# Two-layer hybrid decoder on one core: SwiGLU chunks in the order 2,4,4,4,4,4 instead of 4,4,4,4,4,2, with the gate tiles in a pool of their own

## The chip, the cores and the metric

The kernel runs on one core of one Trainium2 chip, as one program with one launch. The metric is device time in microseconds (us) from the start to the end of an execution; lower is better. The engines are named as in the profile: PE is the matmul engine (TensorE), PEld its weight loads, DVE is VectorE, ACT is ScalarE, POOL is GpSimd, and SP is SyncE, whose queue (SPq) issues nearly all DMA transfers here. psd, psy, wl, xL and the like are names of tiles in the program.

## The reference, cut to what matters

Two layers (DEPTH = 2) act on a prompt of 1024 tokens and on 8 sample tokens with the same weights. In each layer a projection of the normalised activations feeds differential attention and gated linear attention (GLA); both are run over the prompt, and for the 8 samples as a decode step over 64 pages of a key and value cache and a GLA state. Then follow the output projection and the part that the change is in:

```python
x = x + concat(attention, gla) @ w_out              # 1024 -> 1024
n = rmsnorm(x, norm2)
g, u = split(n @ w_gu)                              # 1024 -> 2 x 2816
x = x + (silu(g) * u) @ w_down                      # 2816 -> 1024
```

After the second layer x is written out as y_prompt and y_sample. Inputs, weights and outputs are float32. The kernel splits each float32 operand into a rounded high part and a remainder (wh and wl, hh and hl, xH and xL) and sums three matmuls, high by high, high by low and low by high.

## The kernel before

**Layout.** Activations lie features by tokens: x is 8 tiles (index j) of 128 features x 1032 tokens. The second part of a layer is done in two halves of the tokens: X = 0 has 512 prompt tokens, X = 1 the other 512 and the 8 sample tokens (520 columns, done as two matmuls of 260 columns). Each half runs `out_half` (output projection, residual, next x) and then `ffn_half`. While X = 0 runs, `decode` is interleaved with it: pages of the cache are loaded (`load_page`), multiplied on POOL (tile page) and summed on DVE (tile sall).

**The FFN.** The 2816 = 22 x 128 hidden rows are handled in chunks. `gates(c)` computes silu of the gate part into a tile sa, `ups(c)` multiplies the up part by it and leaves a pair of activation tiles hh and hl for each 128 rows, `down(c)` multiplies these by w_down and adds the result to acc. The chunks are pipelined: ups(c), gates(c+1), down(c); the last ups stands before the second-last down, so that the last two downs run back to back. PE sums into the pool psD of two buffers (psd); for X = 0 one buffer holds a pair of j, for X = 1 one j. One j of a down needs 3 matmuls of 512 columns for each 128 rows of the chunk (6 of 260 for X = 1), one cast of its weight block to wh on ACT and one subtraction to wl on DVE (`prep_tile`, three raw, three wh and two wl buffers), and, once per psd, the addition acc<-psd,acc on DVE.

**What stands at the end of a half.** In the last down of layer 0 each finished j goes to `new_x`: xH on ACT, xL on DVE, a square on ACT, and its addition to ssq on POOL. In the last down of layer 1 each finished j goes out instead: four transposes on PE (psy), a copy on ACT into yall, and a 256 KB store on SP (L1074). yall uses the place of sa, and ysall that of tb (same tags, one buffer each).

**The next half.** `out_half` for X = 1 loads two tiles oHa and oLa (1 MB each, SP, L967) and makes two more, oHb and oLb, from og on ACT and DVE. They are 128 x 2080 floats each, and the three matmuls of each of the eight k use b tiles first and a tiles second.

**What sets the order.** Calls carry a planned time (`dense`, `mix`), from which the build orders the instructions of each engine; an engine then runs its list in order, and each instruction waits for its inputs and for the place it writes to. A pool opened where a closed one lay takes over the same memory, and its tiles wait until the old tiles' last readers are done (reuse_waits); of a store the last reader is the transfer itself. The pool fp (sa, tb, hh, hl) stays open for X = 0 until out_half of X = 1 is done (`fctx`), while acc and the decode's tiles are closed right after X = 0 (`actx`).

Of the kernel before, what the change touches and what calls it, by code (L numbers as in the profile page):

```python
# [10 lines left out]
F32 = mybir.dt.float32  # L11
F32R = mybir.dt.float32r
# [50 lines left out]
def hybrid_kernel(  # L63
# [201 lines left out]
    def layer(l):  # L265
        sn = smp.tile([NB, 2 * H], F32, name="sn", tag="sn")
        osf = smp.tile([P, 2 * H, NB], F32, name="osf", tag="osf")
        smc = smp.tile([P, 2, 3, NB], F32, name="smc", tag="smc")
        gsm = smp.tile([P, H, NB], F32, name="gsm", tag="gsm")
        if l:  # L270
            sample_cols()

        with ExitStack() as octx:
            with ExitStack() as mix_:
                pgp = mix_.enter_context(tc.tile_pool(name="pgp", bufs=1, reuse_waits="tile", side="right"))
                with ExitStack() as dctx:
                    wa2 = phase_d(l, dctx, sn, pgp)
                ogb = octx.enter_context(tc.tile_pool(name="ogb", bufs=1, reuse_waits="tile"))
                og1 = ogb.tile([P, H, WM], F32, name="og1", tag="og1")
                oga = octx.enter_context(ExitStack())  # L280
                ogp = oga.enter_context(tc.tile_pool(name="oga", bufs=1, reuse_waits="tile"))
                og0 = ogp.tile([P, H, HALF], F32, name="og0", tag="og0")
                ogs = (og0, og1)
                with ExitStack() as gctx:
                    phase_g(l, gctx, ogs, smc, gsm, wa2)
            with ExitStack() as pctx:
                psD = pctx.enter_context(tc.tile_pool(name="psD", bufs=2, space=PSUM, reuse_waits="tile"))
                psn = pctx.enter_context(tc.tile_pool(name="psn", bufs=2, space=PSUM, reuse_waits="tile"))
                psX = pctx.enter_context(tc.tile_pool(name="psX", bufs=2, space=PSUM, reuse_waits="tile"))
                wps = [pctx.enter_context(tc.tile_pool(name=n, bufs=1, reuse_waits="tile", side="right")) for n in ("wFr", "wFh", "wFl")]  # L290
                span_start()
                with ExitStack() as fctx:
                    with ExitStack() as actx:
                        ac = new_acc(actx)
                        cp = actx.enter_context(tc.tile_pool(name="dec", bufs=1, reuse_waits="tile", side="right"))
                        acc = out_half(l, 0, og0, osf, ac, wps, psD)
                        oga.close()
                        ffn_half(l, 0, acc, ac, wps, psD, psn, fctx)
                        clock["mix"] = MIX_START
                        decode(l, cp, osf, smc, gsm, psX)  # L300
                    actx = pctx.enter_context(ExitStack())
                    ac = new_acc(actx)
                    acc = out_half(l, 1, og1, osf, ac, wps, psD)
                ffn_half(l, 1, acc, ac, wps, psD, psn, actx)
                span_end()

    def load_page(dst, src, idx):
# [685 lines left out]
                    new_x(acc, ac, X, j, g2c[:, l, j:j + 1])  # L993
        return acc

    def ffn_half(l, X, acc, ac, wps, psD, psn, st):
        W = COLS[X]
        t0 = X * HALF
        last = l == DEPTH - 1
        fp = st.enter_context(tc.tile_pool(name="fp", bufs=1, reuse_waits="tile"))  # L1000
        xh = lambda k: xH[:, k, t0:t0 + W]
        xl = lambda k: xL[:, k, t0:t0 + W]
        chunks = [list(range(c, min(c + 4, NF))) for c in range(0, NF, 4)]
        r = rstd[:, t0:t0 + W].unsqueeze(1)

        def gates(c):
            sa = fp.tile([P, 4, WM], F32, name="sa", tag="sa", bufs=1)
            for fs in groups(X, chunks[c]):
                ps = psD.tile([P, 2, 512], F32, name="psd", tag="d")
                for u, ff in enumerate(fs):  # L1010
                    dense(5.6)
                    ws = prep_tile(wps, w_gu[l, :, ff * P:(ff + 1) * P], KD)
                    gemm3(unit_outs(ps, X, u), *ws, xh, xl, range(KD))
                if fs[0] == 0:
                    rms_half(X, psn)
                n = len(fs)
                i0 = fs[0] - chunks[c][0]
                tt(unit_view(sa[:, i0:i0 + n, :W], X, n), unit_ps(ps, X, n),
                   unit_view(bc(r, [P, n, W]), X, n), ALU.mult)
            n = len(chunks[c])  # L1020
            last_silu.append(act(sa[:, :n, :W], sa[:, :n, :W], AF.Silu))
            if X == 0 or c == len(chunks) - 1:
                load_ln_exp()
            return sa

        def ups(c, sa):
            hs = []
            for fs in groups(X, chunks[c]):
                ps = psD.tile([P, 2, 512], F32, name="psd", tag="d")
                for u, ff in enumerate(fs):  # L1030
                    dense(5.6)
                    ws = prep_tile(wps, w_gu[l, :, DFF + ff * P:DFF + (ff + 1) * P], KD)
                    gemm3(unit_outs(ps, X, u), *ws, xh, xl, range(KD))
                n = len(fs)
                i0 = fs[0] - chunks[c][0]
                g = 2 if X == 0 else 1
                tb = fp.tile([P, g, W], F32, name="tb", tag="tb", bufs=1)[:, :n, :]
                tt(unit_view(tb, X, n), unit_ps(ps, X, n), unit_view(bc(r, [P, n, W]), X, n), ALU.mult)
                tt(tb, tb, sa[:, i0:i0 + n, :W], ALU.mult)
                hh = fp.tile([P, g, W], F32R, name="hh", tag="hh", bufs=6 // g)[:, :n, :]  # L1040
                hl = fp.tile([P, g, W], F32R, name="hl", tag="hl", bufs=6 // g)[:, :n, :]
                act(hh, tb, AF.Copy)
                tt(hl, tb, f(hh), ALU.subtract)
                for u in range(n):
                    hs.append((hh[:, u, :], hl[:, u, :]))
            return hs

        def down(c, hs):
            fs = chunks[c]
            end = c == len(chunks) - 1  # L1050
            if end and last:
                yall = fp.tile([P, 4, WM], F32, name="yall", tag="sa", bufs=1)
                ysall = fp.tile([P, 2 if X == 0 else 1, W], F32, name="ysall", tag="tb", bufs=1)
            for js in groups(X, list(range(KD))):
                ps = psD.tile([P, 2, 512], F32, name="psd", tag="d")
                for u, j in enumerate(js):
# [37 lines left out]
    def decode(l, cp, osf, smc, gsm, psX):  # L1094
# [25 lines left out]
        def sample_gla(p):  # L1120
            q, k, eg = (smc[:, p, a, :] for a in range(3))
            sh = [P, 4, DV]
            vbs = []
            for b0 in (0, 4):
                bs = slice(b0, b0 + 4)
                S0 = cp.tile(sh, F32, name="S0", tag="S0", bufs=1)
                vb = cp.tile(sh, F32, name="vb", tag="vb", bufs=2)
                mix(5)
                with behind(1):
                    for e in range(2):  # L1130
                        h = 2 * p + e
                        SP.dma_start(S0[64 * e:64 * e + 64], state_gla[l, bs, h].rearrange("b d v -> d b v"))
                        SP.dma_start(vb[64 * e:64 * e + 64],
                                     scr_gv[l][bs, h * DV:(h + 1) * DV].unsqueeze(0).to_broadcast([64, 4, DV]))
                tt(S0, S0, bc(eg[:, bs].unsqueeze(2), sh), ALU.mult, POOL)
                tt(vb, vb, bc(k[:, bs].unsqueeze(2), sh), ALU.mult, POOL)
                tt(S0, S0, vb, ALU.add, POOL)
                with tc.issue_after(mark_at(clock["mix"] + 10)[1].ins):
                    for e in range(2):
                        SP.dma_start(gla_sample[l, bs, 2 * p + e].rearrange("b d v -> d b v"), S0[64 * e:64 * e + 64])  # L1140
                tt(vb, S0, bc(q[:, bs].unsqueeze(2), sh), ALU.mult, POOL)
                vbs.append(vb)

            def out():
                ps = psx("pss")
                pv = ps[:, 0:16].rearrange("p (b e) -> p b e", e=2)
                for b in range(NB):
                    mm(pv[:, b, :], vbs[b // 4][:, b % 4, :], hsel, True, True)
                DVE.tensor_copy(osf[:, H + 2 * p:H + 2 * p + 2, :], pv.rearrange("p b e -> p e b"))

            return out

        def decode_softmax():
# [27 lines left out]
            for j in range(NPG):  # L1181
                mm(pw[:, j * 32:(j + 1) * 32], pe_[j // 4][:, (j % 4) * P:(j % 4 + 1) * P], sel, True, True)
            act(wall, pw[:, 0:256].rearrange("p (j c) -> p j c", c=32), AF.Copy)
            wn = cp.tile([64, P], F32, name="dwn", tag="wn")
            DVE.tensor_copy(wn, bc(sm[:, 2:3], [64, P]))
            pn = psx("psn2")
            mm(pn[:, 0:32], wn, sel, True, True)
# [145 lines left out]
```

## Time and profile before

| | us |
|---|---|
| device time, median of 3 runs | 2788.39 (2784.14 to 2790.25) |
| device time of the profiled execution | 2795.14 |
| its span, first to last instruction | 2793.3 |
| PE busy | 2709.5 (97%) |
| DVE busy | 1824.9 (65%) |
| ACT busy | 1358.8 (49%) |
| POOL busy | 403.0 (14%) |
| mean granted TensorE clock | 0.989 |

The span starts with the first instruction, and all stamps below count from there; 1.8 us of the profiled execution lie around it. In it the last down of X = 0 ends near 974 us in layer 0 and near 2355 us in layer 1; those of X = 1 end near 1415 us and at the end of the span. A row of windows gives the stretch, its length, the busy time (and count) of PE, PEld, DVE, ACT and POOL, the granted TensorE clock (1.00 is 2.4 GHz, 0.50 is 1.2 GHz), the DMA engines' busy share and GB/s.

### The profile page before, as it was taken

How to read it: one execution, taken by the hardware profiler on the slowest of the kernel's cores; microseconds unless marked ns; L12 is line 12 of the kernel's file. 1: busy time of each engine (PE TensorE's matmuls, PEld its weight loads, DVE VectorE, ACT ScalarE, POOL GpSimd, SP SyncE). 2: the span in 40 equal slices, each digit the busy share in tenths (PEclk: the TensorE clock that was granted, in tenths of full speed). 3: DMA queues.
4: the chain of work that ended last, by engine and by line, in shares of the span. 5: the costliest groups of instructions: out<-in, count | busy, mean ns of one | idle time of the engine just before them, and what ended most of it. 6: DMA issues, size and time to landing. Idle time of an engine off the chain costs nothing.

```text
span 2793.3 us, 46822 instructions
## 1 busy us (share of the span) xinstructions
PE 2709.5 (97%) x16906; PEld 2403.9 (86%) x16906; DVE 1824.9 (65%) x3549; ACT 1358.8 (49%) x3343; POOL 403.0 (14%) x333
## 2 busy tenths in 40 slices
PE   8999999999999999999999999999999999999999
PEld 6888788777888799999988878877788888999999
DVE  6777676788777664444477775777777775544444
ACT  7888545533454442222278884455324454322222
POOL 1000100145343100000020001002453430000000
PEclk9999999999999999999999999999999999999999
DMA  5111111356666342333212111124566665333332
GB/s 133 56 56 41 57 32 54 109 176 201 185 200 195 104 128 84 93 94 94 75 42 70 47 38 49 32 59 137 174 202 177 191 192 151 91 92 91 91 91 84
DMA packets 461322, 298.13 MB, mean 107 GB/s; under 512 B 34698, under 2 KB 416906, under 8 KB 461090
## 3 DMA queue, kind: packets, MB, share of 16 engines
q1 hardware_dynamic: 452322, 290.90, 35.4%
q10 hardware_dynamic: 8704, 4.20, 0.6%
q8 instruction: 134, 2.20, 0.3%
q14 instruction: 98, 0.80, 0.1%
q0 software_dynamic: 64, 0.03, 0.0%
HBM read 271.53 MB, written 23.53 MB: 106 GB/s over the span
## 4 chain that ended last, share of the span: by engine, by line
PE 78%; DVE 10%; ACT 8%; issue 2%; DMA 2%; SPq 0%; POOL 0%; ACTq 0%; DVEq 0%; POOLq 0%
PE psd L82 56%; PE psq L82 4%; PE psqk L82 3%; PE psv L82 3%; PE psgg L82 2%; PE po L82 2%; ACT sc L88 2%; PE psA L82 1%; DVE wl L135 1%; PE psS L82 1%; ACT qn L88 1%; PE poG L82 1%; ACT qhh L88 1%; PE tpw L85 1%; DVE acc L135 1%
## 5 line engine op out<-in xcount | busy, mean ns | idle before, releaser
L88 ACT ACTIVATE wh<-raw 128x512 fp32r<-128x512 f32 (+1 forms) x608 | 353.6, 615 | 909.3 <-PE psd L82 737.3
L82 PE MATMUL psd<-xH,wh 128*128 128x260 f32 (+1 forms) x2112 | 681.9, 323 | 3.6 <-ACT xH L88 3.5
L82 PE MATMUL psd<-xL,wh 128*128 128x260 f32 (+1 forms) x2112 | 679.9, 322 | 4.2 <-DVE xL L138 4.2
L82 PE MATMUL psd<-xH,wl 128*128 128x260 f32 (+1 forms) x2112 | 682.2, 323 | 0.9 <-DVE wl L135 0.9
L135 DVE TENSOR_TENSOR wl<-raw,wh 128x512 fp32r<-128x512 f32 (+1 forms) x608 | 443.9, 746 | 72.8 <-issue 41.3
L82 PEld LDWEIGHTS psd<-xL,wh 128*128 128x128 f32 x2112 | 400.2, 189 | 38.4 <-DVE xL L138 6.5
L82 PEld LDWEIGHTS psd<-xH,wh 128*128 128x128 f32 x2112 | 399.8, 189 | 36.3 <-ACT xH L88 4.4
L82 PEld LDWEIGHTS psd<-xH,wl 128*128 128x128 f32 x2112 | 400.3, 190 | 34.2 <-DVE wl L135 1.8
L82 PE MATMUL psd<-hh,wl 128*128 128x260 f32 (+1 forms) x1056 | 340.6, 323 | 6.1 <-DVE wl L135 6.0
L82 PE MATMUL psd<-hh,wh 128*128 128x260 f32 (+1 forms) x1056 | 338.8, 321 | 0.9 <-DVE acc L135 0.9
L82 PE MATMUL psd<-hl,wh 128*128 128x260 f32 (+1 forms) x1056 | 338.3, 320 | 0.0
L135 POOL TENSOR_TENSOR page<-page,qbd 128x512 f32<-128x512 f32 x128 | 190.5, 1504 | 307.9 <-DMA page<-in_cache_k 162.7
L135 DVE TENSOR_TENSOR acc<-psd,acc 128x520 f32<-128x520 f32 (+1 forms) x144 | 125.6, 872 | 150.7 <-PE psd L82 150.7
L82 PEld LDWEIGHTS psd<-hh,wl 128*128 128x128 f32 x1056 | 199.1, 189 | 25.8 <-DVE wl L135 12.0
L82 PEld LDWEIGHTS psd<-hh,wh 128*128 128x128 f32 x1056 | 199.2, 189 | 14.6 <-issue 1.3
L82 PEld LDWEIGHTS psd<-hl,wh 128*128 128x128 f32 x1056 | 198.8, 188 | 13.6
L82 PE MATMUL psq<-wh,xH 128*128 128x384 f32 (+1 forms) x512 | 180.0, 352 | 7.3 <-DVE zs L135 4.3
L135 DVE TENSOR_TENSOR sa<-psd,rstd 128x520 f32<-128x520 f32 (+1 forms) x66 | 57.7, 874 | 197.0 <-PE psd L82 194.7
L82 PE MATMUL psq<-wh,xL 128*128 128x384 f32 (+1 forms) x512 | 179.4, 351 | 0.0
L82 PE MATMUL psq<-wl,xH 128*128 128x384 f32 (+1 forms) x512 | 178.6, 349 | 0.0
L135 DVE TENSOR_TENSOR tb<-psd,rstd 128x520 f32<-128x520 f32 (+1 forms) x66 | 57.7, 874 | 165.9 <-PE psd L82 165.9
L138 DVE SCALAR_TENSOR_TENSOR wl<-raw,g1c,wh 128x256 fp32r<-128x256 f32 (+2 forms) x160 | 80.9, 536 | 73.5 <-ACT wh L88 72.8
(330 smaller groups left out, 5421.2 us busy)
## 6 DMA issues: line engine op xcount, KB each, us to landing
raw<-in_w_gu SPq DMA_DIRECT2D x176, 512.0 KB
raw<-in_w_down SPq DMA_DIRECT2D x160, 256.0 KB
page<-in_cache_k SPq DMA_DIRECT2D x128, 256.0 KB
page<-in_cache_v SPq DMA_DIRECT2D x128, 256.0 KB
raw<-in_w_out SPq DMA_DIRECT2D x32, 512.0 KB
raw<-in_w_in SPq DMA_DIRECT2D x64, 192.0 KB
raw<-in_w_in SPq DMA_DIRECT2D x64, 128.0 KB
xt<-in_x_prompt SPq DMA_DIRECT2D x8, 512.0 KB
```

Of the source, the lines that this page charges most:

```text
L82: PE.matmul(out, lhsT=lhsT, rhs=rhs, start=start, stop=stop, skip_group_check=True)
L85: PE.matmul(out, lhsT=in_, rhs=ident[:n, :n], is_transpose=True)
L88: return ACT.activation(out, in_, func, **kw)
L135: return (eng or DVE).tensor_tensor(out, a, b, op=op)
L138: (eng or DVE).scalar_tensor_tensor(out=out, in0=in0, scalar=scalar, in1=in1, op0=op0, op1=op1)
```

## The change

The chunk of 2 x 128 rows, which was the last, becomes the first; the last two downs are both 4 x 128 rows deep. As the last two chunks of activations are held together, hh and hl have room for eight 128-row tiles instead of six. sa and tb (and with them yall and ysall) move from fp to a new pool fs, which for X = 0 is closed with actx, so before out_half of X = 1, and lies above fp. In decode the state S0 and the small tile dwn take slots of the tag page (five buffers) instead of places of their own. The matmuls, the weights loaded, and the other transfers are the same in number and size, except that the 128 x 256 weight blocks come first.

```diff
-                        ffn_half(l, 0, acc, ac, wps, psD, psn, fctx)
+                        ffn_half(l, 0, acc, ac, wps, psD, psn, fctx, actx)
...
-                ffn_half(l, 1, acc, ac, wps, psD, psn, actx)
+                ffn_half(l, 1, acc, ac, wps, psD, psn, actx, actx)
...
+        fs_ = st2.enter_context(tc.tile_pool(name="fs", bufs=1, reuse_waits="tile"))
...
-        chunks = [list(range(c, min(c + 4, NF))) for c in range(0, NF, 4)]
+        chunks = [list(range(max(0, c), c + 4)) for c in range(NF % 4 - 4, NF, 4)]
...
-            sa = fp.tile([P, 4, WM], F32, name="sa", tag="sa", bufs=1)
+            sa = fs_.tile([P, 4, WM], F32, name="sa", tag="sa", bufs=1)
...
-                hh = fp.tile([P, g, W], F32R, name="hh", tag="hh", bufs=6 // g)[:, :n, :]
+                hh = fp.tile([P, g, W], F32R, name="hh", tag="hh", bufs=8 // g)[:, :n, :]
...
-                yall = fp.tile([P, 4, WM], F32, name="yall", tag="sa", bufs=1)
+                yall = fs_.tile([P, 4, WM], F32, name="yall", tag="sa", bufs=1)
...
-                S0 = cp.tile(sh, F32, name="S0", tag="S0", bufs=1)
+                S0 = cp.tile([P, 512], F32, name="S0", tag="page", bufs=NPB).rearrange("p (b d) -> p b d", b=4)
```

**DVE, layer 0, the last down of X = 0.** Before, from the third addition to acc to the first two subtractions of the next output projection (wl<-raw,wh 128x512):

```order
L135 TENSOR_TENSOR acc<-psd,acc 128x2x512
L135 TENSOR_TENSOR xL<-acc,xH 128x512
L135 TENSOR_TENSOR wl<-raw,wh 128x256
L135 TENSOR_TENSOR xL<-acc,xH 128x512
L135 TENSOR_TENSOR wl<-raw,wh 128x256
L135 TENSOR_TENSOR xL<-acc,xH 128x512
L135 TENSOR_TENSOR acc<-psd,acc 128x2x512
L135 TENSOR_TENSOR wl<-raw,wh 128x256
L135 TENSOR_TENSOR xL<-acc,xH 128x512
```

The same stretch now, up to the last addition to acc:

```order
L135 TENSOR_TENSOR acc<-psd,acc 128x2x512
L135 TENSOR_TENSOR wl<-raw,wh 128x512
L135 TENSOR_TENSOR xL<-acc,xH 128x512
L135 TENSOR_TENSOR wl<-raw,wh 128x512
L135 TENSOR_TENSOR xL<-acc,xH 128x512
L135 TENSOR_TENSOR wl<-raw,wh 128x512
L135 TENSOR_TENSOR acc<-psd,acc 128x2x512
L135 TENSOR_TENSOR wl<-raw,wh 128x512 x2
L135 TENSOR_TENSOR xL<-acc,xH 128x512 x2
```

The same kinds of instruction alternate, but the weight blocks are twice as wide and one subtraction for the output projection has moved ahead of the last addition to acc.

**SP, layer 1, the end of X = 0.** Names in brackets are what the instruction waits for: DMAHW with a number is the landing of an earlier transfer, the others are engines. Before, the loads of oHa and oLa stand among the loads for the last down, and the stores of y (out<-yall) come behind them:

```order
L900 DMA raw<-in_w_down 128x2x128 [waits DMAHW6_49,DVE_49,Activation_49]
L967 DMA oHa<-scr_oh_110 128x4x512 [waits PE_49,Pool_49]
L900 DMA raw<-in_w_down 128x2x128 [waits DMAHW7_49,DVE_49,Activation_49]
L967 DMA oLa<-scr_ol_114 128x4x512
L900 DMA raw<-in_w_down 128x2x128 [waits DMAHW0_49,DVE_49,Activation_49]
```

Now the last two stores and what follows them:

```order
L1075 DMA out<-yall 128x4x128 [waits Activation_49]
L1075 DMA out<-yall 128x4x128 [waits DMAHW4_49,Activation_49]
L900 DMA raw<-in_w_out 128x8x128 [waits DMAHW6_49,DMAHW5_49,DVE_49]
L967 DMA oHa<-scr_oh_110 128x4x512 [waits DMAHW3_49,DMAHW4_49,DMAHW1_49,DMAHW0_49]
L967 DMA oLa<-scr_ol_114 128x4x512 [waits DMAHW7_49,PE_49,Pool_49]
L900 DMA raw<-in_w_out 128x8x128 [waits DVE_49]
```

oHa and oLa have moved behind all eight stores of y, and oHa waits for the landing of the last four. In layer 0 (no stores there) the two loads keep their place among the loads for the last down, and oHa waits for nothing.

**PE, the same place.** Now, from the last matmul of the last down over the last transposes to the first matmul that reads oHa (20 more rows of oHb and oLb lie between the two pieces):

```order
L82 MATMUL psd<-hl,wh 128x512
L82 MATMUL psd<-hh,wl 128x512
L85 MATMUL psy<-ident,acc 128x128 x8
L82 MATMUL psd<-oHb,wh 128x260 x2
L82 MATMUL psd<-oLb,wh 128x260
```

```order
L82 MATMUL psd<-oHb,wl 128x260
L82 MATMUL psd<-oHa,wh 128x260
L82 MATMUL psd<-oLb,wh 128x260
L82 MATMUL psd<-oHb,wl 128x260
```

Before, the last eight transposes stood behind the first 12 matmuls of the next output projection; now they follow the last down at once. One matmul reads oHa after 24 of oHb and oLb; 23 more of these follow, and then the rest on oHa and oLa.

## Rows read from the trace of the kernel before

**Rows 1.** The page: span, busy time, chain of work that ended last.

```profile
span 2793.3 us, 46822 instructions
...
PE 2709.5 (97%) x16906; PEld 2403.9 (86%) x16906; DVE 1824.9 (65%) x3549; ACT 1358.8 (49%) x3343; POOL 403.0 (14%) x333
...
PE 78%; DVE 10%; ACT 8%; issue 2%; DMA 2%; SPq 0%; POOL 0%; ACTq 0%; DVEq 0%; POOLq 0%
```

**Rows 2.** Windows, end of X = 0 in layer 0.

```profile
964.00:970.00 6.00, 4.49 (x19) 3.00 (x18) 5.77 (x7) 4.38 (x10) 3.40 (x3) 1.00 0.41 120
970.00:984.00 14.00, 9.11 (x32) 6.98 (x31) 11.56 (x12) 7.83 (x14) 6.11 (x5) 0.51 0.41 118
984.00:990.00 6.00, 6.00 (x52) 6.00 (x51) 2.59 (x5) 2.00 (x4) 0.00 (x0) 1.00 0.30 89
```

**Rows 3.** PE's groups by form, 964 to 984 us: busy, mean ns, idle before.

```profile
L82 PE MATMUL psd<-hh,wl 128*128 128x512 f32 x9 | 4.6, 512 | 2.2 <-DVE wl L135 2.2
L82 PE MATMUL psd<-hl,wh 128*128 128x512 f32 x9 | 4.2, 466 | 0.0
L82 PE MATMUL psd<-hh,wh 128*128 128x512 f32 x8 | 3.6, 453 | 0.0
```

**Rows 4.** The chain of waits, 955 to 990 us: start, length, what.

```profile
954.83 9.58 PE psd L82 x41
...
977.26 2.28 DVE wl L135 x2
```

**Rows 5.** Timeline of DVE in the last down: start, length, what.

```profile
966.89 0.41 DVE L135 TENSOR_TENSOR wl<-raw,wh 128x256 fp32r<-128x256 f32 x1
967.22 1.77 DVE L135 TENSOR_TENSOR xL<-acc,xH 128x512 fp32r<-128x512 f32 x1
...
970.94 1.21 DVE L135 TENSOR_TENSOR acc<-psd,acc 128x1024 f32<-128x1024 f32 x1
...
972.85 0.69 DVE L135 TENSOR_TENSOR xL<-acc,xH 128x512 fp32r<-128x512 f32 x1 [0.37 <-ACT xH L88]
```

**Rows 6.** Timeline of POOL in the same stretch.

```profile
967.16 1.29 POOL L135 TENSOR_TENSOR ssq<-ssq,nsq 128x512 f32<-128x512 f32 x1 [0.74 <-ACT nsq L88]
```

**Rows 7.** Windows, end of X = 1 in layer 0.

```profile
1396.00:1404.00 8.00, 7.71 (x62) 7.28 (x60) 6.10 (x10) 4.34 (x9) 1.44 (x1) 1.00 0.22 66
1404.00:1416.00 12.00, 9.19 (x63) 8.17 (x63) 11.08 (x15) 6.70 (x12) 7.10 (x6) 1.00 0.48 109
```

**Rows 8.** DVE's groups by form, 1404 to 1416 us.

```profile
L135 DVE TENSOR_TENSOR xL<-acc,xH 128x520 fp32r<-128x520 f32 x6 | 7.2, 1202 | 0.9 <-ACT xH L88 0.9
```

**Rows 9.** Timeline of SP's queue, layer 1: start and length of issuing.

```profile
2331.86 0.42 SPq L967 DMA_DIRECT2D oHa<-scr_oh  x1
...
2333.75 0.46 SPq L967 DMA_DIRECT2D oLa<-scr_ol  x1
...
2358.99 0.92 SPq L1074 DMA_DIRECT2D out<-yall  x2
...
2790.01 0.37 SPq L1074 DMA_DIRECT2D out<-yall  x1
```

**Rows 10.** Windows over the two loads and over the last store.

```profile
2332.00:2342.00 10.00, 10.00 (x46) 8.24 (x45) 7.18 (x14) 3.83 (x10) 0.00 (x0) 1.00 0.82 262
...
2790.00:2792.00 2.00, 0.00 (x0) 0.00 (x0) 0.00 (x0) 0.00 (x0) 0.00 (x0) 1.00 0.47 133
```

**Rows 11.** Timeline of PE, end of X = 0 in layer 1.

```profile
2356.80 1.03 PE L85 MATMUL psy<-ident,acc 128*128 128x128 f32 x8
```

**Rows 12.** Timeline of ACT, the same place.

```profile
2358.39 1.06 ACT L88 ACTIVATE yall<-psy 128x512 f32<-128x512 f32 x2
```

**Rows 13.** PE's waits, 2340 to 2375 us: total, times, longest.

```profile
PE psd L82 <- DVE wl L135: 0.3, 1, 0.3
```

**Rows 14.** DVE's groups by form, 640 to 690 us, beside decode in layer 0.

```profile
L135 DVE TENSOR_TENSOR wl<-raw,wh 128x512 fp32r<-128x512 f32 x18 | 18.7, 1058 | 2.4 <-issue 2.4
L1115 DVE TENSOR_REDUCE sall<-page 128x8 f32<-128x512 f32 x18 | 12.0, 678 | 5.0 <-POOL page L135 5.0
```

More of the change, by code (lines that the diff above doesn't have):

```diff
@@ L994, in out_half, with ffn_half @@
         return acc
-    def ffn_half(l, X, acc, ac, wps, psD, psn, st):
+    def ffn_half(l, X, acc, ac, wps, psD, psn, st, st2):
         W = COLS[X]
@@ L1036, in ups @@
                 g = 2 if X == 0 else 1
-                tb = fp.tile([P, g, W], F32, name="tb", tag="tb", bufs=1)[:, :n, :]
+                tb = fs_.tile([P, g, W], F32, name="tb", tag="tb", bufs=1)[:, :n, :]
                 tt(unit_view(tb, X, n), unit_ps(ps, X, n), unit_view(bc(r, [P, n, W]), X, n), ALU.mult)
                 tt(tb, tb, sa[:, i0:i0 + n, :W], ALU.mult)
-                hh = fp.tile([P, g, W], F32R, name="hh", tag="hh", bufs=6 // g)[:, :n, :]
-                hl = fp.tile([P, g, W], F32R, name="hl", tag="hl", bufs=6 // g)[:, :n, :]
+                hh = fp.tile([P, g, W], F32R, name="hh", tag="hh", bufs=8 // g)[:, :n, :]
+                hl = fp.tile([P, g, W], F32R, name="hl", tag="hl", bufs=8 // g)[:, :n, :]
                 act(hh, tb, AF.Copy)
@@ L1051, in down @@
             if end and last:
-                yall = fp.tile([P, 4, WM], F32, name="yall", tag="sa", bufs=1)
-                ysall = fp.tile([P, 2 if X == 0 else 1, W], F32, name="ysall", tag="tb", bufs=1)
+                yall = fs_.tile([P, 4, WM], F32, name="yall", tag="sa", bufs=1)
+                ysall = fs_.tile([P, 2 if X == 0 else 1, W], F32, name="ysall", tag="tb", bufs=1)
             for js in groups(X, list(range(KD))):
@@ L1183, in decode_softmax @@
             act(wall, pw[:, 0:256].rearrange("p (j c) -> p j c", c=32), AF.Copy)
-            wn = cp.tile([64, P], F32, name="dwn", tag="wn")
+            wn = cp.tile([P, 512], F32, name="dwn", tag="page", bufs=NPB)[0:64, 0:P]
             DVE.tensor_copy(wn, bc(sm[:, 2:3], [64, P]))
```

## The prediction

> **What bounds the kernel now.** The page comes first: PE is busy 2709.5 of 2793.3 us, and the chain that ended last is PE for 78% and DVE for 10% [rows 1]. The change adds and removes no matmul, so it can only give or take idle time of PE, 84 us in all, and time at the lower clock. So I went to the places where a short chunk meets DVE or where a freed buffer is waited for, and read there the windows (how much PE lost), the chain and the waits (to whom), and the timelines (how long each instruction is).
>
> Two numbers carry the arithmetic. Undisturbed, 41 matmuls of 512 columns take 9.58 us [rows 4], 0.234 us each; 52 of 260 columns take 6.00 us [rows 2], 0.115 us each. A pair of j in a down of X = 0 has 12 of the first in a 2-deep chunk and 24 in a 4-deep one, so 2.80 or 5.61 us; a j of X = 1 takes 1.38 or 2.77 us.
>
> In the last down of layer 0, X = 0, DVE needs for such a pair two wl of 0.41, one addition of 1.21 and two xL of 0.69 [rows 5], together 3.4 us against PE's 2.80. It is worse in practice: POOL adds to ssq meanwhile, 1.29 us each [rows 6], and the xL beside it takes 1.77 instead of 0.69 [rows 5], which makes up to 5.6 us. PE waits for wl [rows 3], then for two wl of the output projection that stand behind these xL and took 2.28 us [rows 4], and the granted clock is 0.51 from 970 to 984 us [rows 2], nearly all of it at the lower level of 1.2 GHz.
>
> **Term 1, the end of X = 0 in layer 0: a gain of 10 us (8 to 11).** From 964 to 984 us PE did 19 + 32 = 51 matmuls [rows 2], 26 of them of 512 columns [rows 3]. At full clock without waits these are 26 x 0.234 + 25 x 0.115 = 9.0 us; 20 went by, so 11.0 were lost. With four rows a pair gives PE 5.61 us, while DVE needs two wl of 128x512 (0.69 each, like the xL of the same shape), one addition and two xL: 4.0 us with POOL idle, 6.1 if every xL takes 1.77. POOL's two adds cover less than half of the pair, so I take about 5.1, under PE's. The last pair still leaves its xL between the subtractions of the output projection: 1 us (0 to 3).
>
> **Term 2, the end of X = 1 in layer 0: a gain of 4 us (3 to 5.5).** From 1396 to 1416 us there are 62 + 63 matmuls [rows 7], nearly all of 260 columns; at 0.115 they are 14.4 us of 20, so up to 5.6 were lost. DVE's xL took 1.20 us on the mean [rows 8]; with one wl of 0.41 and one addition of about 0.7 this is 2.3 us for each j against PE's 1.38. Afterwards it is 0.7 + 0.7 + 1.2 = 2.6 against 2.77. DVE just fits, and POOL's last additions to ssq, which the next layer's norm waits for, come as late as before, counted from the last matmul: I keep back 1.5 us.
>
> **Term 3, the end of X = 0 in layer 1: a loss of 9.3 us (6.5 to 14).** Here there is no xL, and PE lost 0.3 us [rows 13]. oHa and oLa were issued at 2331.86 and 2333.75, over 20 us before they were needed [rows 9]. Now they take the memory of yall, and oHa waits on SP until the last four stores have landed. Count from E, the end of the last down on PE. DVE's addition takes 1.21 [rows 5], the eight transposes 1.03 [rows 11], the two copies to yall 1.06 [rows 12]; the second store is issued about E + 3.7. The kernel's last store moved its 266 KB within 2 us (133 GB/s) of its issue [rows 9, 10], so oHa is issued near E + 6. For the loads, the stretch with both moved 262 GB/s over 10 us [rows 10]; 2.1 MB at that rate take 8.0 us, so oLa lands at E + 14. Meanwhile PE has the transposes and 48 matmuls on oHb and oLb, 1.03 + 5.52 = 6.6 us; the row of oHa among them only splits the wait in two. That leaves PE idle for 7.4 us. The clock falls after such waits: at 0.51 the 32 matmuls of 970 to 984 us took some 4.5 us more [rows 2]. Here this may cost 0 to 4.5; I take 1.9, since PE restarts with a long run of ready work. Queued behind oHa on SP are only oLa and weights that are not next.
>
> The Trainium skill (DMA: Bandwidth & Descriptors, Anatomy of one DMA) gives a transfer 2.0 us fixed, mostly the wait until the last byte is confirmed, and 436 GB/s, fitted on another issuing path. By it the store would take 2.6 us and the two loads together 6.8, oLa would land at E + 13.1, and the sum below would be 2.6 us faster instead of 1.7. The rows' 262 GB/s, which include other transfers and the start, agree in size with it.
>
> **Term 4, the first down beside decode: a loss of 3 us (0 to 6).** The first down is now 2 deep while pages are processed. Its four pairs give PE 11.2 us. DVE needs 8 x 0.41 + 4 x 1.21 = 8.1 [rows 5] and, at 18 page sums in 50 us of 0.68 each [rows 14], 2.7 more: 10.8, about full. Beside POOL a wl took 1.06 instead of 0.69 [rows 14]; eight such excesses of 0.37 are 3.0 us, which would overflow by 2.6. So 0 to 3 for each layer; I take 1.5. What hides the lower figure is the lead of three casts that ACT has on PE.
>
> **Term 5, the slots of tag page, the transfers' order, and the tail: 0 (1 gained to 2 lost).** S0 takes a page's slot for a moment while four others stay. At the end of the kernel the y work for each j is the same and PE still has the same total.
>
> **Sum.** 10 + 4 - 9.3 - 3 = 1.7 us gained. The profiled execution, 2795.14 us, would become 2793.4, 0.06% less; it ran 6.75 above the median of 2788.39, and 0.06% off that median gives 2787. A measurement of this kernel can tell about 0.2%, 5.6 us, from no change.
>
> **Rivals.**
>
> *The loads are quick: faster.* SP's queue is emptier after E than at 2332 us. At twice the rate, oLa lands at E + 10; the idle time is 3.4 us and perhaps the clock holds. Then 10 + 4 - 3.4 - 3 = 7.6: 2781. Against it stands 262 GB/s with the DMA engines 82% busy [rows 10], for which I see no reason to double.
>
> *The loads are late: slower.* Stores, weights of w_out at 512 KB each and the two loads share the queue; each such weight block in front costs 0.5 / 0.262 = 2 us. With three in front oLa lands at E + 20, the idle time is 13.4 us and the clock adds 4.5: 10 + 4 - 17.9 - 3 = -6.9, 2795. It decides (slower by 5.6) from a loss of 16.6 us at this place, so from oLa near E + 19. Against it: SP's order shows one block between the last store and oHa.
>
> *DVE stays the bound in layer 0: the change doesn't do what it says.* If every xL waits out a whole addition on POOL, a pair costs DVE 2 x 0.69 + 1.21 + 2 x (0.69 + 1.29) = 6.55 us against 5.61, 2.8 us over three pairs; in X = 1 a j costs 3.4 against 2.77, and term 2 vanishes. Then 7.2 - 9.3 - 3 = -5.1: 2793.5. The longest xL so far, 1.77 [rows 5], is under the 1.98 of this case. The Trainium skill (SBUF — State Buffer, Who interferes with whom) has a VectorE instruction with two SBUF inputs and a GpSimd one that reads SBUF exclude each other for a whole instruction; the xL of 1.77 beside an add of 1.29 agrees with that in kind.
>
> **How the numbers follow.** The forecast, within 5.6 us of before, gets 0.40; quick loads 0.30; late loads 0.14; DVE as the bound 0.16, of which 0.10 within 0.2% and 0.06 slower. So faster 0.30, same 0.50, slower 0.20. The terms' better ends give 11 + 5.5 - 6.5 = 10 us, 2778, and the worse 8 + 3 - 14 - 6 = -9, 2797; with the rest of term 5 I set 2777 to 2797.
>
> **What the changed profile would show.** Term 1: around 965 to 985 us the clock stays at 1.00 and PE's waits for wl are under 3 us. Term 2: the waits for wl and acc near 1400 to 1415 us are gone. Term 3: in layer 1, oHa is issued behind the last out<-yall, PE waits for it and then for oLa for 6 to 10 us, with a window of low clock behind. Term 4: short waits for wl near 640 us and at the like place of layer 1. A loss at the start of a half's FFN, or in decode beyond 6 us, would make the forecast wrong; so would a clock that falls for much longer than PE waits.

## The result and the profile after

The change makes the kernel slower: 2807.64 us median (2799.18 to 2810.94, 6 runs) against 2789.01 (2784.14 to 2791.75, 6 runs), a ratio of 1.006 with a 95% interval of 1.0045 to 1.0075. The profiled execution took 2803.0 us, 7.9 more than that of before; that of before lay above all of its timed runs and that of the changed kernel at the fast side of its own, so sizes below are taken from ratios of runs, and the traces say where.

The head of the page of the changed kernel, against [rows 1]:

```profile
span 2800.1 us, 46812 instructions
...
PE 2710.3 (97%) x16906; PEld 2399.8 (86%) x16906; DVE 1806.0 (64%) x3549; ACT 1357.4 (48%) x3343; POOL 389.6 (14%) x333
...
PE 76%; DVE 10%; ACT 8%; DMA 3%; issue 2%; POOL 1%; SPq 0%; ACTq 0%; DVEq 0%; POOLq 0%
```

PE did the same work in the same busy time; of the chain that ended last, DMA and POOL each have one point more than before. The windows of the changed kernel, in time order (columns as in [rows 2]):

```profile
624.00:648.00 24.00, 20.27 (x76) 14.62 (x76) 18.57 (x23) 9.33 (x14) 9.72 (x7) 0.93 0.71 207
700.00:714.00 14.00, 11.03 (x43) 8.58 (x42) 8.65 (x11) 2.94 (x5) 8.57 (x6) 0.88 0.79 244
...
928.00:976.00 48.00, 48.00 (x222) 39.47 (x221) 32.12 (x48) 20.85 (x41) 6.91 (x5) 1.00 0.47 142
...
1396.00:1404.00 8.00, 8.00 (x69) 8.00 (x68) 5.30 (x8) 4.14 (x7) 3.89 (x5) 1.00 0.67 140
```

The lower two rows are the gains. The last 48 us of X = 0 in layer 0 are without a gap and at clock 1.00, where before lost 11.0 us [rows 2]; the end of X = 1 is full as well, where [rows 7] has 62 matmuls in the same stretch. The upper two are new losses beside the page sums of decode, in and just behind the first down and in the second. At 0.234 us each the 76 and 43 matmuls need 17.8 and 10.1 us; 24 and 14 went by, so 10.1 us were lost, in layer 0 alone. Layer 1 has the like: from the last matmul of X = 0's output projection to the last of its FFN, by PE's stamps, 406.7 us went by (from 1948.0 to 2354.7) where before took 396.3 (from 1958.3 to 2354.6), so 10.4 us were lost there.

The chain of waits of the changed kernel around the second (start, length, what) shows how:

```profile
697.60 0.39 SPq L900
...
700.45 5.30 DMA page<-in_cache_k
...
705.91 1.30 POOL page L135
...
707.23 0.07 DVE sall L1116
...
707.83 1.22 DVE acc L135
709.05 1.13 DVE wl L135
...
710.22 2.08 PE psd L82 x4
```

SP issues the page behind a weight load that waited for a raw buffer; the page takes 5.30 us to land, POOL multiplies it in 1.30, and only then can DVE do the sum. The addition to acc and the wl that PE waits for stand behind that sum in DVE's list. PE stood 3.0 us, for 2.6 of which DVE was idle as well.

The third loss is in layer 1, the end of X = 0. Chain of waits of the changed kernel, then PE's waits from 2340 to 2375 us (total, times, longest):

```profile
2354.73 1.23 DVE acc L135
...
2357.26 0.60 ACT yall L88
...
2357.87 3.11 DMA out<-yall
...
2361.07 5.39 DMA oHa<-scr_oh
...
2366.50 8.56 PE psd L82 x69
```

```profile
PE psd L82 <- DMA oHa<-scr_oh: 3.2, 1, 3.2
PE psy L85 <- DVE acc L135: 1.4, 1, 1.4
PE psd L82 <- ACT oHb L88: 1.3, 1, 1.3
```

The last store lands 3.11 us after the copy, then oHa is issued and takes 5.39. PE is idle for 5.9 us in three pieces, where it lost 0.3 [rows 13].

### The profile page after: what moved, and what is told of

It reads as the page before. It is cut to its first block, busy times and chain, and to the rows that moved or that the text cites. A ratio compares the mean times of both kernels' runs of the same rounds, so it can differ in the third digit from the quotient of the medians.

```text
span 2800.1 us, 46812 instructions
## 1 busy us (share of the span) xinstructions
PE 2710.3 (97%) x16906; PEld 2399.8 (86%) x16906; DVE 1806.0 (64%) x3549; ACT 1357.4 (48%) x3343; POOL 389.6 (14%) x333
## 4 chain that ended last, share of the span: by engine, by line
PE 76%; DVE 10%; ACT 8%; DMA 3%; issue 2%; POOL 1%; SPq 0%; ACTq 0%; DVEq 0%; POOLq 0%
PE psd L82 56%; PE psq L82 4%; PE psqk L82 3%; PE psv L82 3%; PE psgg L82 2%; PE po L82 2%; ACT sc L88 2%; DVE wl L135 1%; PE psS L82 1%; ACT qn L88 1%; DVE acc L135 1%; DMA raw<-in_w_in 1%; PE psA L82 1%; ACT qhh L88 1%; PE poG L82 1%
## 5 line engine op out<-in xcount | busy, mean ns | idle before, releaser
L88 ACT ACTIVATE wh<-raw 128x512 fp32r<-128x512 f32 (+1 forms) x608 | 353.8, 614 | 894.0 <-PE psd L82 678.2
L135 DVE TENSOR_TENSOR wl<-raw,wh 128x512 fp32r<-128x512 f32 (+1 forms) x608 | 452.5, 760 | 75.3 <-issue 25.1
```

Source lines behind the costliest of these rows:

```text
L88: return ACT.activation(out, in_, func, **kw)
L135: return (eng or DVE).tensor_tensor(out, a, b, op=op)
```

## The experiments

All ratios are to the kernel before, run on the same chip. Theory A: the ends in layer 0 give what was forecast, and the late oHa and the short chunk beside decode take more than that. Its rivals are that the ends give nothing (B), that pools and page slots disturb decode (C), and that DVE simply has too much work beside the short chunk (D).

**two_before_last**: kernel before, one line.

```diff
-        chunks = [list(range(c, min(c + 4, NF))) for c in range(0, NF, 4)]
+        chunks = [list(range(s, s + n)) for s, n in ((0, 4), (4, 4), (8, 4), (12, 4), (16, 2), (18, 4))]
```

> The kernel before with one edit: chunks of 4,4,4,4,2,4, so that the last chunk is 4 deep, the first stays 4 deep, never more than six activation tiles are held, and all pools stay as they were. Theory A (the short first chunk beside decode and the late oHa load cost what the ends in layer 0 give): only the gains are left. PE lost about 12 us at the end of X = 0 and about 4 us at the end of X = 1 in layer 0 before; so 14 to 16 us faster than before, near 2774 us, the clock at 1.00 from 965 to 985 us, and oHa issued early in layer 1. Rival B (the gains were never there, since DVE and POOL bound the end of a half either way): within 3 us of before.

Measured: 2782.36 us, ratio 0.9962 (0.9951 to 0.9974), 10.6 us faster. B falls. It is less than 14 to 16, and the trace shows a part of the rest. PE's waits from 930 to 980 us:

```profile
PE psd L82 <- DVE wl L135: 3.0, 2, 1.6
PE psd L82 <- ACT wh L88: 0.3, 1, 0.3
```

None of this lies in the down of the short chunk itself, now the second-last. 1.4 us stand at the third matmul of the last down (946.7), whose first wl comes on DVE behind two subtractions to oLb and the short chunk's last addition; the 0.3 follow in the same down. 1.6 us stand behind the last down, in the next output projection (971.0), whose wl come behind the xL of the last pair; the prediction's term 1 had set 1 us aside for these. oHa is issued at 2310.11 us there, ahead of the stores of y.

**pools_only**: changed kernel, old order of chunks.

```diff
-        chunks = [list(range(max(0, c), c + 4)) for c in range(NF % 4 - 4, NF, 4)]
+        chunks = [list(range(s, s + n)) for s, n in ((0, 4), (4, 4), (8, 4), (12, 4), (16, 4), (20, 2))]
```

> The changed kernel with the chunks back in the order 4,4,4,4,4,2; the pool fs, the room for eight activation tiles and the shared page slots stay. Theory A: only the late oHa load is left, in layer 1: PE idle for some 6 us at the end of X = 0 there, with a short stretch at the low clock; 6 to 9 us slower than before, near 2797 us, and decode as before. Rival C (the shared page slots or the new pool disturb decode): 15 to 20 us slower than before, with stalls of PE in layer 0 beside decode.

Measured: 2805.4 us, ratio 1.0045 (1.0032 to 1.0059), 12.5 us slower. The place is the one that A names, but the size is more than 6 to 9. PE's waits from 2340 to 2400 us, then windows over the same place:

```profile
PE psd L82 <- ACT oHb L88: 3.4, 1, 3.4
PE psd L82 <- DMA oHa<-scr_oh: 3.3, 1, 3.3
PE psy L85 <- DVE acc L135: 2.3, 1, 2.3
```

```profile
2356.00:2366.00 10.00, 5.22 (x26) 4.79 (x26) 2.81 (x6) 3.38 (x8) 0.00 (x0) 0.67 0.90 286
2366.00:2374.00 8.00, 8.00 (x46) 8.00 (x47) 0.00 (x0) 0.00 (x0) 0.00 (x0) 0.66 0.22 84
```

9.0 us of waits, and a clock of 0.67 and 0.66 for 18 us, in which much of the work ran at 1.2 GHz. C is not borne out: layer 0 beside decode has no new stall (PE's wait for wl from 574 to 930 us is 0.4 us, 1.6 before).

**y_in_h_slots**: changed kernel, yall moved off sa's place (core of the edit).

```diff
-                yall = fs_.tile([P, 4, WM], F32, name="yall", tag="sa", bufs=1)
...
+                    ty = ("hh", "hl")[js[0] // g % 2]
+                    yall = f(fp.tile([P, g, W], F32R, name="yall", tag=ty, bufs=8 // g))
```

> The changed kernel with yall in free slots of hh and hl instead of the place of sa, so that oHa needs not wait for the stores of y; chunks 2,4,4,4,4,4. Theory A: the wait for oHa in layer 1 goes, 6 to 8 us faster than the changed kernel, near 2800 us, and the stalls beside decode stay. Rival: the load of oHa moves early, but collides with weights of the last down, and only 0 to 3 us come back.

Measured: 2796.71 us, ratio 1.0013 (1.0000 to 1.0027), 0.47% or 13 us less than the changed kernel. SP's queue there has both loads early again, and PE has no wait from 2340 to 2375 us:

```profile
2331.86 0.50 SPq L967 DMA_DIRECT2D oHa<-scr_oh  x1
...
2357.75 1.09 SPq L1078 DMA_DIRECT2D out<-yall  x2
```

Two opposite edits give 12.5 us (9 to 16) and 13 us (some 6 either way) for the wait on the stores. The traces have it at the same place: from the end of the last down of X = 0 in layer 1 to the end of the next output projection, PE took 47.9 us before, 55.2 in the changed kernel, 61.0 in pools_only and 47.1 in y_in_h_slots.

**sums_later**: changed kernel, the order of one instruction (and mark_at kept within the list of marks).

```diff
-                with behind(3, 1):
+                with behind(3, -1):
                     DVE.tensor_reduce(out=sall[:, j, b, :], in_=pg.rearrange("p (h d) -> p h d", d=DK), axis=AX.X, op=ALU.add)
```

> The changed kernel with the page sums on DVE (sall) ordered two weight blocks later, nothing else. Theory A, in its finer form (a page is loaded a fixed number of weight blocks ahead of its sum; with blocks of 1.4 us instead of 2.8 or 5.6 us the page is not there, DVE stands at the sum, and the wl and acc behind it are late): the stalls beside decode near 630 to 645 and 707 us mostly go, 12 to 20 us faster than the changed kernel, near 2790 us. Rival D (DVE has too much work there, whatever the order): within 4 us of the changed kernel.

Measured: 2795.69 us, ratio 1.0016 (1.0003 to 1.0029), 0.44% or 12 us less than the changed kernel, with some 6 us of doubt either way. The stall near 707 us is gone, but those near 630 and 638 us only in part. D is no full answer, since the work is the same. DVE's idle time before sall in layer 0, from the group of this tile, in the changed kernel:

```profile
its engine sat idle before it (us, times) until:
  POOL page L135: 11.1, 7
```

In sums_later there is no such wait. In the kernel before it is 5.0 us, 4 times.

**before_sums_later** and **before_sums_earlier**: kernel before, the same instruction put two weight blocks later (-1) or one earlier (2).

```diff
-                with behind(3, 1):
+                with behind(3, 2):
```

> The kernel before with the page sums on DVE ordered two weight blocks later, chunks 4,4,4,4,4,2: a control for the same edit on the changed kernel. Lead theory (what costs is a page that is not there when DVE comes to its sum): before has only one such stall in a layer, of 1 us, so 0 to 3 us faster than before. If the later sums are worth 8 us or more here as well, what they gave the changed kernel says nothing about the short chunk.

> The kernel before with the page sums ordered one weight block earlier, chunks 4,4,4,4,4,2. Lead theory: the lead of a page over its sum shrinks by a third, the stalls that the changed kernel shows appear without any short chunk, above all in the downs beside decode; 8 us or more slower than before, with PE waiting for wl behind a sum that waits for POOL. Rival (the amount of DVE work beside a short chunk costs, not the lead): within 3 us of before.

Measured: later 2792.01 us, ratio 1.0003 (0.9991 to 1.0015), no change; so the edit is worth 12 us beside a short first chunk and nothing without one. Earlier 2804.0 us, ratio 1.0040 (1.0027 to 1.0054), 11 us slower, with no short chunk beside decode. DVE's idle time before sall is then

```profile
its engine sat idle before it (us, times) until:
  POOL page L135: 36.6, 23
```

The downs were expected to lose most. In layer 0 the FFN of X = 0 as a whole took no longer (397.2 us, 400.6 before); PE lost its time in the output projection in front of it. Windows there, before and in before_sums_earlier:

```profile
550.00:575.00 25.00, 21.79 (x91) 16.59 (x90) 25.00 (x29) 9.61 (x16) 14.39 (x10) 1.00 0.63 200
```

```profile
550.00:575.00 25.00, 19.02 (x73) 14.13 (x72) 20.68 (x25) 7.17 (x12) 14.26 (x9) 0.93 0.69 212
```

In layer 1 the FFN of X = 0 took 4.7 us longer. So the lead of a page can cost without a short chunk, but DVE's idle time is no price by itself: 27.7 of the 36.6 us lie from 580 to 720 us, beside the 4-deep chunks, where PE's waits for wl are 3.3 us, 0.9 before.

**two_second**: changed kernel with the order 4,2,4,4,4,4.

```diff
-        chunks = [list(range(max(0, c), c + 4)) for c in range(NF % 4 - 4, NF, 4)]
+        chunks = [list(range(s, s + n)) for s, n in ((0, 4), (4, 2), (6, 4), (10, 4), (14, 4), (18, 4))]
```

> The changed kernel with chunks 4,2,4,4,4,4: the short chunk is the second, still beside the page sums of decode. Lead theory: the down of the short chunk stalls there too, PE and DVE as in the changed kernel; about as slow as the changed kernel, 8 to 17 us slower than before. Rival (it is the start, where the first down follows the gates early, that costs): only the late oHa load and the gains of the ends are left, near 2795 us, 0 to 4 us slower than before.

Measured: 2806.8 us, ratio 1.0052 (1.0034 to 1.007), as slow as the changed kernel. So it is not the very start that costs: a short second chunk beside the key pages costs as much. PE's waits there, 572 to 930 us, are again on casts and wl, ACT's wh most of all:

```profile
PE psd L82 <- ACT wh L88: 4.2, 2, 3.3
PE psd L82 <- DVE wl L135: 2.0, 3, 0.9
```

**pools_two_before_last**: changed kernel with the order 4,4,4,4,2,4 (the line of two_before_last).

> The changed kernel's pools with chunks 4,4,4,4,2,4: no short chunk beside the page sums, but oHa behind the stores of y. If the terms add: minus 0.38% (measured for this order on the old pools) plus 0.45% (measured for the pools alone), so within 0.15% of before, near 2793 us, with decode as before. If the late load costs less behind a 4-deep last down, 0.2% faster than before.

Measured: 2795.33 us, ratio 1.0009 (0.9999 to 1.0019): minus 0.38% and plus 0.45% add.

**two_first_both_mended**: the edits of y_in_h_slots and sums_later together.

> The changed kernel, chunks 2,4,4,4,4,4, with both mends: yall in free slots of hh and hl (no wait of oHa for the stores) and the page sums two weight blocks later. If the two losses are independent and are all that stands against the gains at the ends: the 0.6% of the change, less 0.47% for the stores, less 0.44% for the sums, so 0.2 to 0.4% faster than before, near 2783 us. If moving one stall only makes room for the other, it stays within 0.1% of before.

Measured: 2787.87 us, ratio 0.9980 (0.9969 to 0.9991), faster by 5.6 us, at the low edge of 0.2 to 0.4%. Within the noise the two losses add, but they are not all: short stalls at the first down remain. The chain of waits of sums_later there, which has the same first down:

```profile
625.98 0.42 ACT wh L88
...
626.42 1.28 ACT L88
...
627.71 1.00 ACT sa L88
...
629.65 1.28 ACT L128
...
630.94 0.43 ACT wh L88
```

The silu of the chunk just computed and the two function table loads around it stand between two casts on ACT for 4.5 us (L88 without a tile and L128). Four rows to a chunk give a block of weights every 2.8 us of PE, two rows every 1.4, so three wh in hand last 4.2 us, less than the 4.5.

**before_no_page_sums** and **two_first_no_page_sums**: the kernel before and y_in_h_slots, each without decode's key pages: their loads, the load of the query, the products and the sums are left out, and sall is set to zero, so y_sample and what hangs on it are not computed from the cache.

```diff
             for j in range(NPG):
                 mix(2.6)
-                pg = page(cache_k[l], b, j)
-                tt(pg, pg, qb, ALU.mult, POOL)
-                with behind(3, 1):
-                    DVE.tensor_reduce(out=sall[:, j, b, :], in_=pg.rearrange("p (h d) -> p h d", d=DK), axis=AX.X, op=ALU.add)
```

> The kernel before without decode's key pages: their loads, POOL's products and DVE's sums are left out (sall is set to zero), decode over the value pages stays; chunks 4,4,4,4,4,2. A base for the next run. Both theories: 0 to 4 us faster than before, since the key pages cost it only short stalls.

> Chunks 2,4,4,4,4,4 with yall in slots of hh and hl (no wait of oHa for the stores), and without decode's key pages as in the run beside it. Theory E (beside the page sums the short first down loses time by itself: its casts stand behind silu and two table loads on ACT, and the wl of the next gates have 1.4 us of cover): the waits of PE near 630 and 638 us stay, and it is 4 to 10 us faster than the base without key pages. Rival (all that the short first down costs comes from the pages): these waits go, and the ends in layer 0 show whole, 13 to 16 us faster than that base.

Measured: 2769.75 us, ratio 0.9910 (0.9895 to 0.9924), and 2762.7, ratio 0.9880 (0.9863 to 0.9896). The first is 24 us faster than before, not 0 to 4: a miss, told of at the end. The second is 7 us faster than the first, inside 4 to 10; of theory E's two waits one is there and one is not. PE's one wait from 590 to 650 us is

```profile
PE psd L82 <- ACT wh L88: 0.9, 1, 0.9
```

so the wait on ACT near 626 us is the short chunk's own, while the longer ones near 638 us came from the pages. The wait alone understates what is lost: in the profile a matmul of 512 columns takes 0.39 us and the next starts after 0.23, so a pause shorter than this overlap does not show. The windows of a stretch that holds the first down of layer 1 in two_first_no_page_sums, first in before_no_page_sums, then in that kernel:

```profile
1985.00:2000.00 15.00, 15.00 (x66) 12.14 (x65) 7.29 (x9) 4.25 (x7) 0.00 (x0) 1.00 0.31 92
```

```profile
1985.00:2000.00 15.00, 13.95 (x56) 9.76 (x55) 9.13 (x14) 8.02 (x11) 0.00 (x0) 1.00 0.55 155
```

Ten matmuls fewer at full clock are 2.3 us, and the whole FFN of X = 0 in layer 1 took 391.2 us against 387.2. In layer 0 the stretch from the end of one output projection to the end of the next took 434.7 us against 442.2, a gain of 7.5 where the end gives 11. So the traces have some 7 us lost with no key page near, and the medians agree (7 us gained, where the ends should give some 15); that they are all the short first down's own is likely but not shown.

**two_before_last_sums_later**: the edits of two_before_last and sums_later on the kernel before.

> Chunks 4,4,4,4,2,4 on the pools of before, with the page sums two weight blocks later: the gains of the ends without the late load and without the sums' waits. 10 to 14 us faster than before, 0 to 3 us faster than the same order of chunks with the sums where they were.

Measured: 2778.52 us, ratio 0.9953 (0.9939 to 0.9966), 13 us faster than before and the fastest of the kernels with the whole of decode.

## Why the prediction was wrong, by its own steps

**Term 1 and term 2 (gains of 10 and 4): right.** The changed kernel has the end of X = 0 without a gap, so 11 us are back in the traces, and the FFN of X = 1 is 4.2 us shorter (381.7 against 385.9). The rival that DVE stays the bound is refuted by the 48.00 us of PE in 48.00.

**Term 3 (a loss of 9.3, 6.5 to 14): right in mechanism and within its range, with its parts mis-sized.** 12.5 and 13 us were measured. "The kernel's last store moved its 266 KB within 2 us" was taken for the time to landing; with w_out's weights and another store in the queue it took 3.11 us, so oHa was issued at E + 6.3 (E + 6 in the forecast). An estimate from the Trainium skill (DMA: Bandwidth & Descriptors, Anatomy of one DMA), whose 2.0 us fixed and 436 GB/s were fitted on another issuing path, gives 2.6 us for a store of this size; the chain's 3.11 decides, and 4.23 in pools_only. oHa itself came sooner than was worked out (E + 11.8 by the chain, where both loads were put at E + 14), and oLa was not waited for, so the idle time was 5.9 us rather than 7.4 in the changed kernel's trace, but 9.0 in that of pools_only. Missed was that the casts to oHb also move behind the copies to yall (1.3 to 3.4 us of PE's wait). For the clock 1.9 us were set aside: the changed kernel's trace has 7.3 us more at this place than before, of which 5.9 were idle; pools_only has 13.1, of which 9.0 were idle, with 18 us at about 0.66.

**Term 4 (a loss of 3, 0 to 6): the step that failed.** It compared DVE's work with PE's time, 10.8 against 11.2 us, found them about equal and took 1.5 us for each layer; the traces show 10.1 us lost in layer 0 and 10.4 in layer 1. The time went elsewhere: the sum of a page stands at a fixed number of weight blocks behind its load, and with blocks of 1.4 us the load is not there in time, so DVE waits with acc and wl behind it. Sums_later takes back 12 us, and before_sums_earlier makes the same kind of wait, and 11 us of loss, without a short chunk. The second down was not in the sum at all, and PE stood 3.0 us there. The casts behind silu and table loads on ACT were not in it either; the "lead of three casts" that it counted on lasts 4.2 us against their 4.5. With both mends the kernel is still 9 us behind the 15 or so that the traces give the ends, and some 7 us are lost without key pages too, so most of this does not come from the pages. How it divides between ACT's casts, the pages near 638 us and the clock was not measured by itself. The prediction had named a loss "in decode beyond 6 us" as a sign that it would be wrong, and this is what came.

**Term 5: held.** pools_only has no new stall beside decode.

Together: 15 gained at the ends, 12.5 lost to the stores, 12 to the sums and some 9 to the short first down give 18 us slower; 17 were measured by the ratio, 18.6 by the medians. The 9 is itself what was left over in two_first_both_mended, so this sum is no proof of it; what speaks for it are the 20.5 us that the traces show lost in the two layers, against 12 + 9. The rival "loads are late" named the right sign and place, but its price was not what decided.

## What to carry to other kernels

A short block at the end of a pipeline can be traded for one elsewhere only after asking what runs beside it there. Where one engine's list interleaves two streams, count the lead of each load over its use in time, not in blocks: halving the block halves the lead. Count in time also how long the weights cast in advance last, against the longest other work in that engine's list. A tile that is the source of a store holds its memory until the store has landed, so what is loaded next should not lie there.

## What the runs showed that was not expected

The key pages cost the kernel before 24 us, though PE shows few waits on them. Windows at the start of the gates of X = 0 in layer 0, in the kernel before and in before_no_page_sums:

```profile
574.00:592.00 18.00, 13.59 (x41) 9.68 (x41) 16.71 (x18) 4.64 (x8) 8.90 (x6) 0.72 0.52 163
```

```profile
570.00:588.00 18.00, 18.00 (x87) 14.15 (x86) 10.57 (x17) 7.80 (x14) 0.00 (x0) 1.00 0.33 95
```

With the key pages 41 matmuls were done in 18 us, without them 87. At 0.234 us each the 41 need 9.6 us, so 8.4 were lost in this place alone, which the change did not touch. PE's waits from 560 to 595 us are 5.7 us on xL, xH and wl before, and none beyond 0.2 us without the pages. Which of the pages' loads, products and sums makes xL and xH late was not taken apart.
